# Attention output of a hybrid decoder layer: one 512-column matmul in place of two of 256 columns, and a sum of four quarters after it

## The chip, the core and the metric

The kernel is one program on one NeuronCore of a Trainium2 chip. The core has a matrix engine (PE), a vector engine (DVE), a scalar engine (ACT), a second elementwise engine (POOL) and a queue that issues most transfers (SP). Each runs its own instructions in order and they wait for each other through semaphores. The metric is the time of one execution on the device, in microseconds; lower is better. PE writes its results to PSUM, eight banks of 512 fp32 columns on 128 partitions; DVE and ACT read them from there, and POOL works on SBUF alone in this kernel.

## What is computed

One decoder layer on x (1024 x 1024, fp32): a joint projection to q, k, v (8 heads of 64) and to a gated MLP over chunks, dilated causal attention, an output projection with a layer norm, a feed-forward part with a depthwise convolution, and a gate. The part that the change touches is the attention. The reference forms three dilated windows and merges them by their denominators:

```python
scores = jnp.einsum('bnqrhd,bnkrhd->bnrhqk', qb, kb) * (1.0 / math.sqrt(dh))
scores = jnp.where(mask[None, :, None, None], scores, NEG_INF)
e = jnp.exp(scores - m)
out = jnp.einsum('bnrhqk,bnkrhd->bnqrhd', e / den, vb)
...
wts = jax.nn.softmax(jnp.stack(lses, axis=0), axis=0)
return jnp.einsum('cbsh,cbshd->bshd', wts, jnp.stack(outs, axis=0))
```

The kernel computes the same as one causal attention in which a key that lies in two or three of the windows counts two or three times (a mask that adds log 2 or log 3).

## The kernel before

To keep fp32 precision every operand is split into a high and a low part (`hi` is the value rounded by a copy, `lo` the rest), and products are summed over the parts. A linear layer takes three matmuls for this (`mm3`, L131 to L134). The program order is written out by hand: what a Python loop issues first comes first on its engine.

Attention runs over 32 units, one for each pair of a block I of 256 queries (I = 0 to 3) and a head h. A unit has I + 1 slots, so there are 80 slots. In each slot, in this order, `attention` (L743) issues: the scores of a later unit (`unit_S`, L661: two matmuls at L688 and L689 into a bank "S", of which there are two); on DVE a pass that adds the mask and finds the maximum (L698), and then whatever stands in the list `later`; the exp of a finished unit on ACT (L704) and its normalisation on POOL (L710, L712); four (in the last slot of a unit three) transposes of 128 x 128 probabilities on PE (`unit_T`, L719) into one of three banks, followed by a copy on ACT that makes the high part of the tile `pt` (L111) and, through `later`, a subtraction on DVE that makes its low part (L723); the product with V (`unit_PV`, L545) of the slot three slots back; and some matmuls of another stage (L132 to L134), with DVE work of their own (L637 splits the mixed heads, L650 adds to the residual, L579 and L583 are layer norm statistics).

`unit_PV` takes two key blocks a slot. The weights are V of one head: 64 columns of the high part and 64 of the low part, so partitions 0 to 63 of the output bank "O" hold probabilities times V high, and partitions 64 to 127 probabilities times V low. The moving operand is 256 columns of `pt` (128 for the last key block of a unit, which lies on the diagonal), once for the high and once for the low part, both summed into the same 256 columns of the bank. There are two "O" banks, and a unit holds one from its first slot to the end of its output.

After a unit's last slot `unit_out` (L560) copies one half of the partitions to SBUF with ACT (tile `ot`, L569 by way of L111) and puts a DVE addition of the other half into `later` (L570); it writes into `mixf`. It runs in the next slot, behind that slot's passes at L698 and the subtraction at L723 that were listed before it. `ot` is a tile of its own with one buffer. Most other tiles of the stage (`pt`, `sp`, `qe`, `x`) are pages of 4 KiB a partition out of one pool of 24 (`page`, L67); when no page is free, the first instruction that writes a new one waits for the last reader of the one that comes free next. After the last unit, `wo_up(3)` needs its `mixf` first (L111 and L637, then the matmul at L134), and the feed-forward stage follows.

Of the kernel before, what the change touches and what calls it, by code (L numbers as in the profile page):

```python
# [21 lines left out]
F32 = mybir.dt.float32  # L22
# [3 lines left out]
OP = mybir.AluOpType  # L26
# [25 lines left out]
def hybrid_layer(ctx, tc, x, xT, pT, pos, w_in, ln_z_g, ln_z_b, w_sT, b_sT, w_o,  # L52
# [3 lines left out]
    PE, ACT, DVE, POOL, SP = nc.tensor, nc.scalar, nc.vector, nc.gpsimd, nc.sync  # L56
# [4 lines left out]
    small = ctx.enter_context(tc.tile_pool(name="small", bufs=2))  # L61
# [5 lines left out]
    def page(shape, dt, name):  # L67
        return pool.tile(shape, dt, name=name, tag="pg", bufs=24)

    def wpage(shape, dt, name):  # L70
        return pool.tile(shape, dt, name=name, tag="w", bufs=12)
# [17 lines left out]
    def ps1(tag):  # L89
        if tag == "T":  # L90
            tag = ("D1", "B", "B")[n_t[0] % 3]
            n_t[0] += 1
        if tag == "P":
            return psL[0].tile([128, 512], F32, name=tag, tag=tag, bufs=4)
        if tag in ("S", "O"):
            return psL[0].tile([128, 512], F32, name=tag, tag=tag, bufs=2)
        return psR.tile([128, 512], F32, name=tag, tag=tag, bufs=2 if tag == "B" else 1)
# [11 lines left out]
    def copy(eng, dst, src):  # L109
        if eng is ACT:  # L110
            ACT.activation(dst, src, AF.Copy)  # L111
        else:
            eng.tensor_copy(dst, src)
# [288 lines left out]
    def vs(kb):  # L402
        if kb < 4:
            return VL[:, kb]
        if kb not in VP:
            VP[kb] = page([128, H, 128], F32R, "VP")
        return VP[kb]
# [3 lines left out]
    for j in range(4):  # L411
# [6 lines left out]
        for t in range(2):  # L418
            v = vs(2 * j + t)
# [125 lines left out]
    def unit_PV(I, h, m, pt):  # L545
        st = unit_state[I, h]
        if m == 0:
            st["o"] = ps1("O")
        o = st["o"]
        for kb in (2 * m, 2 * m + 1):  # L550
            full = kb <= 2 * I
            src = (kb - 2 * m) * 256
            osl = o[:, 0:256] if full else o[:, 128:256]
            wd = 256 if full else 128
            v = vs(kb)[:, h, :]
            for hl in range(2):
                PE.matmul(osl, v, pt[:, hl, src:src + wd], start=kb == 0 and hl == 0,
                          stop=kb == 2 * I + 1 and hl == 1)

    def unit_out(I, h):  # L560
        st = unit_state.pop((I, h))
        o = st["o"]
        p, odd = divmod(h, 2)
        if h == 0:
            mixes[I] = wpage([128, 4, 256], F32, "mixf")
        r, r2 = (slice(64, 128), slice(0, 64)) if odd else (slice(0, 64), slice(64, 128))
        ot = small.tile([128, 256], F32, name="ot", bufs=1)
        copy(ACT, ot[r], o[r2, 0:256])
        mix = mixes[I][r, p, :]  # L569
        later.append(lambda: DVE.tensor_tensor(mix, o[r, 0:256], ot[r], OP.add))  # L570

    x1 = {}
    lnp = []
# [156 lines left out]
    later = []  # L730
# [12 lines left out]
    def attention(plan):  # L743
# [5 lines left out]
        def flush(keep):  # L749
            while len(pending) > keep:  # L750
                a = pending.pop(0)
                unit_PV(*a)
                if a[2] == a[0]:
                    outs.append(a[:2])

        for n in range(-3, len(units)):
# [8 lines left out]
            for m in range(banks):  # L765
                take = -(-len(news) // (banks - m))
                ttrs = [unit_S(*units[v], ch) for v, ch in news[:take]]
                for f in ttrs + later:
                    f()
                later.clear()  # L770
                for d in [d for d in due if d[0] <= slot]:
                    due.remove(d)
                    d[2]()
                for v, ch in news[:take]:
                    if ch[3]:
                        due.append((slot + 1, "e", lambda v=v, p=ch[0]: unit_exp(*units[v], p)))
                        if ch[0] == 1:
                            due.append((slot + 2, "n", lambda v=v: unit_norm(*units[v])))
                news = news[take:]
                if n >= 0:  # L780
                    I, h = units[n]
                    pt = unit_T(I, h, m)
                    pending.append((I, h, m, pt))
                    flush(3)
                if posts and slot >= posts[0][0] and posts[0][1] in q_toks:
                    later.append(q_post(*posts.pop(0)[1:]))
                pump(rate[0])
                for o in outs:
                    unit_out(*o)
                outs.clear()  # L790
                advance()
                slot += 1
# [4 lines left out]
        for o in outs:  # L797
            unit_out(*o)
# [621 lines left out]
```

## Time and profile before

| | |
|---|---|
| median of three runs | 1275.75 us |
| the three runs | 1273.85, 1275.75, 1277.27 us |
| span of the profiled execution | 1273.2 us |
| attention in it | from about 266 to 466 us |
| busy share of the span: PE, PE weight load | 97%, 79% |
| busy share: DVE, ACT, POOL | 69%, 40%, 53% |
| DMA | 103 GB/s over the span |

The span runs from the first to the last instruction of the profiled execution; what lies around it is not in the trace. That execution lies at the fast end of the three timed runs. Matmuls are pipelined, and the duration shown for one reaches beyond the start of the next, so the cost of a matmul in a row of them is read from start to start. The number behind "x" on a row counts instructions that were merged into it; the bracket names the engine's idle time before the row and what ended it.

### The profile page before, as it was taken

What the parts mean: (1) busy time and instruction counts of PE and PEld (TensorE: products, weight loads), DVE (VectorE), ACT (ScalarE), POOL (GpSimd) and SP (SyncE); (2) the same over time, 40 slices, a digit from 0 to 9 for tenths busy, and PEclk for the clock granted to TensorE, in tenths of its full rate; (3) what the DMA queues carried; (4) which work ended last, traced back from release to release, by engine and by line L of the source; (5) the groups of instructions that cost most, each with busy time, mean ns of one, the idle gap of its engine ahead of it and who ended that gap; (6) DMA issues with size and microseconds to landing.
All of it is one profiled execution on the core that took longest, in us unless ns stands there. A gap on an engine that the chain in (4) does not pass through costs nothing. (4 is left out here: it accounts for less than half of the span.)

```text
span 1273.2 us, 15840 instructions
## 1 busy us (share of the span) xinstructions
PE 1236.7 (97%) x5804; PEld 1003.4 (79%) x5804; DVE 883.4 (69%) x1227; ACT 504.4 (40%) x855; POOL 672.9 (53%) x550
## 2 busy tenths in 40 slices
PE   9999999999999997999999999999999899989997
PEld 6888888877777777888888888888877688868886
DVE  4544422356887788777777777877779977797766
ACT  5322122366866563433333333333343344531221
POOL 2500001254737679467666767666664565783444
PEclk9999999999999998999999999999999999999998
DMA  7115511000201031033212333213688344530001
GB/s 268 67 50 181 182 53 46 34 17 1 84 34 67 34 132 67 34 124 124 93 55 101 124 125 124 100 53 129 206 279 296 104 124 156 191 124 34 34 34 50
DMA packets 61007, 131.71 MB, mean 103 GB/s; under 512 B 5377, under 2 KB 23169, under 8 KB 60929
## 3 DMA queue, kind: packets, MB, share of 16 engines
q1 hardware_dynamic: 58480, 122.17, 28.1%
q10 hardware_dynamic: 2448, 8.52, 2.1%
q8 instruction: 46, 0.75, 0.2%
q14 instruction: 33, 0.26, 0.1%
HBM read 97.90 MB, written 32.77 MB: 103 GB/s over the span
## 5 line engine op out<-in xcount | busy, mean ns | idle before, releaser
L117 POOL TENSOR_TENSOR aop<-raw,aop 128x512 fp32r<-128x512 f32 x77 | 117.6, 1537 | 81.3 <-ACT aop L111 81.2
L132 PE MATMUL P<-xop,wop 128*128 128x512 f32 (+1 forms) x360 | 138.8, 386 | 0.0
L134 PE MATMUL P<-xop,wop 128*128 128x512 f32 (+1 forms) x360 | 138.4, 384 | 0.0
L133 PE MATMUL P<-xop,wop 128*128 128x512 f32 (+1 forms) x360 | 138.4, 384 | 0.0
L117 POOL TENSOR_TENSOR wop<-s,wop 128x512 fp32r<-128x512 f32 x44 | 64.0, 1464 | 96.3 <-ACT wop L111 96.3
L117 DVE TENSOR_TENSOR bop<-wd,bop 128x512 fp32r<-128x512 f32 x66 | 85.2, 1302 | 25.8 <-ACT bop L111 25.7
L117 POOL TENSOR_TENSOR wop<-raw,wop 128x512 fp32r<-128x512 f32 x64 | 82.8, 1300 | 30.9 <-ACT wop L111 30.7
L429 POOL TENSOR_TENSOR rt<-tok,cos_t 128x128 f32<-128x128 f32 x8 | 4.7, 585 | 176.4 <-ACT tok L488 165.2
L133 PE MATMUL P<-bop,aop 128*128 128x512 f32 x176 | 71.3, 405 | 11.7 <-DVE bop L117 11.6
L111 ACT ACTIVATE wop<-s 128x512 fp32r<-128x512 f32 x44 | 26.8, 630 | 138.5 <-DVE s L936 72.3
L132 PEld LDWEIGHTS P<-xop,wop 128*128 128x128 f32 x360 | 67.7, 188 | 13.4
L134 PEld LDWEIGHTS P<-xop,wop 128*128 128x128 f32 x360 | 67.6, 188 | 13.4
L133 PEld LDWEIGHTS P<-xop,wop 128*128 128x128 f32 x360 | 67.7, 188 | 13.3
L111 ACT ACTIVATE aop<-raw 128x512 fp32r<-128x512 f32 x77 | 48.1, 625 | 74.9 <-DMA raw<-hid_d 41.9
L117 POOL TENSOR_TENSOR wop<-wraw,wop 128x512 fp32r<-128x512 f32 x44 | 73.2, 1690 | 6.4 <-ACT wop L111 4.0
L134 PE MATMUL P<-bop,aop 128*128 128x512 f32 x176 | 70.2, 399 | 3.0 <-POOL aop L117 3.0
L132 PE MATMUL P<-bop,aop 128*128 128x512 f32 x176 | 69.7, 396 | 0.0
L1022 POOL TENSOR_TENSOR ht<-ht,ct 128x1024 f32<-128x1024 f32 x22 | 63.1, 2866 | 3.9 <-ACT ht L1019 3.9
L132 PE MATMUL B<-xop,wop 128*128 128x512 f32 x160 | 62.2, 389 | 0.0
L133 PE MATMUL B<-xop,wop 128*128 128x512 f32 x160 | 62.2, 389 | 0.0
L134 PE MATMUL B<-xop,wop 128*128 128x512 f32 x160 | 62.2, 389 | 0.0
L698 DVE CUSTOM_DVE_ANT_0 sp<-S,mask 128x512 f32<-128x512 f32 (+2 forms) x64 | 37.0, 589 | 35.6 <-PE S L689 31.7
(322 smaller groups left out, 3625.7 us busy)
## 6 DMA issues: line engine op xcount, KB each, us to landing
raw<-hid_d SPq DMA_DIRECT2D x35, 512.0 KB, 3.9
hid_d<-ct SPq DMA_DIRECT2D x22, 512.0 KB, 5.2
wd<-in_w_down_dram SPq DMA_DIRECT2D x44, 256.0 KB, 5.1
raw<-in_w_in_dram SPq DMA_DIRECT2D x18, 512.0 KB, 3.7
hid_d<-ht SPq DMA_DIRECT2D x33, 256.0 KB, 5.0
raw<-in_w_a_dram SPq DMA_DIRECT2D x11, 512.0 KB, 3.5
raw<-in_w_b_dram SPq DMA_DIRECT2D x11, 512.0 KB, 4.3
wraw<-in_w_a_dram SPq DMA_DIRECT2D x11, 512.0 KB, 5.2
```

What stands on the lines that cost most here:

```text
L111: ACT.activation(dst, src, AF.Copy)
L117: lo_eng.tensor_tensor(lo, src, hi.bitcast(F32), OP.subtract)
L132: PE.matmul(ps, sh, mh, start=first, stop=False)
L133: PE.matmul(ps, sh, ml, start=False, stop=False)
L134: PE.matmul(ps, sl, mh, start=False, stop=last)
L429: POOL.tensor_tensor(r[:, 0], x1, cb, OP.mult)
L698: DVE.tensor_tensor_reduce(dst, o, mask[:, m0:m0 + w_], op0=OP.add, op1=OP.min, accum_out=acc, scale=-1.0, scalar=prev)
L1022: POOL.tensor_tensor(tt[g, e], tt[g, e], ctile[g, 1, e], OP.mult)
```

## The change

The product of a key block with V becomes one matmul of 2 x 256 columns (2 x 128 on the diagonal): the bank "O" is read as two halves, and the high part of the probabilities goes to columns 0 to 255 and the low part to columns 256 to 511. The two parts are no longer added in PSUM. `unit_out` then has four quarters to add: ACT copies 64 x 512 in place of 64 x 256, DVE adds the other 64 x 512 from PSUM to it in place, and a second DVE addition adds the two halves of 256 columns, both in SBUF. `ot` moves from its own buffer into the pool of pages.

```diff
-        o = st["o"]
+        o = st["o"].rearrange("p (l q) -> p l q", l=2)
         for kb in (2 * m, 2 * m + 1):
             full = kb <= 2 * I
             src = (kb - 2 * m) * 256
-            osl = o[:, 0:256] if full else o[:, 128:256]
             wd = 256 if full else 128
-            v = vs(kb)[:, h, :]
-            for hl in range(2):
-                PE.matmul(osl, v, pt[:, hl, src:src + wd], start=kb == 0 and hl == 0,
-                          stop=kb == 2 * I + 1 and hl == 1)
+            PE.matmul(o[:, :, 256 - wd:256], vs(kb)[:, h, :], pt[:, :, src:src + wd], start=kb == 0,
+                      stop=kb == 2 * I + 1)
...
-        ot = small.tile([128, 256], F32, name="ot", bufs=1)
-        copy(ACT, ot[r], o[r2, 0:256])
+        ot = page([128, 2, 256], F32, "ot").rearrange("p l q -> p (l q)")
+        copy(ACT, ot[r], o[r2])
         mix = mixes[I][r, p, :]
-        later.append(lambda: DVE.tensor_tensor(mix, o[r, 0:256], ot[r], OP.add))
+
+        def join():
+            DVE.tensor_tensor(ot[r], o[r], ot[r], OP.add)
+            DVE.tensor_tensor(mix, ot[r, 0:256], ot[r, 256:512], OP.add)
+        later.append(join)
```

## Rows read from the trace of the kernel before

**Rows 1.** The page's first part: busy time, share and instructions of each engine.

```profile
PE 1236.7 (97%) x5804; PEld 1003.4 (79%) x5804; DVE 883.4 (69%) x1227; ACT 504.4 (40%) x855; POOL 672.9 (53%) x550
```

**Rows 2.** Busy time by stretch of attention: length, PE, PEld, DVE, ACT, POOL, clock, DMA.

```profile
284.00:316.00 32.00, 31.67 (x162) 22.77 (x160) 20.58 (x50) 21.37 (x54) 16.32 (x29) 1.00 0.00 1
316.00:347.00 31.00, 30.75 (x177) 22.73 (x176) 25.69 (x72) 26.52 (x59) 22.79 (x31) 1.00 0.25 86
347.00:391.00 44.00, 44.00 (x231) 32.49 (x231) 33.48 (x79) 25.98 (x49) 18.81 (x25) 1.00 0.07 25
391.00:451.00 60.00, 60.00 (x329) 43.42 (x328) 44.93 (x103) 35.51 (x65) 41.00 (x44) 1.00 0.15 53
451.00:466.00 15.00, 13.61 (x104) 12.34 (x102) 13.85 (x26) 11.13 (x21) 11.41 (x12) 1.00 0.38 136
```

**Rows 3.** Timeline of PE, four places: start and duration in us, instruction.

```profile
359.98 0.48 PE L132 MATMUL D<-wouh,mixh 128*128 128x512 f32 x1
360.30 0.39 PE L133 MATMUL D<-woul,mixh 128*128 128x512 f32 x1
...
429.46 0.65 PE L557 MATMUL O<-pt,VP 128*128 128x256 f32 x4
...
429.95 0.45 PE L132 MATMUL D<-wouh,mixh 128*128 128x512 f32 x1
...
430.24 0.39 PE L133 MATMUL D<-woul,mixh 128*128 128x512 f32 x1
...
434.15 0.72 PE L557 MATMUL O<-pt,VL 128*128 128x256 f32 x4
...
434.71 0.39 PE L132 MATMUL D<-wouh,mixh 128*128 128x512 f32 x1
...
434.94 0.39 PE L133 MATMUL D<-woul,mixh 128*128 128x512 f32 x1
...
477.07 0.28 PE L132 MATMUL P<-xop,wop 128*128 128x256 f32 x1
...
478.38 0.28 PE L134 MATMUL P<-xop,wop 128*128 128x256 f32 x1
```

**Rows 4.** Groups by line and shape, 266 to 465 us: busy us, mean ns, idle before.

```profile
L570 DVE TENSOR_TENSOR mixf<-O,ot 64x256 f32<-64x256 f32 x32 | 13.4, 418 | 1.6 <-ACT ot L111 1.1
L111 ACT ACTIVATE ot<-O 64x256 f32<-64x256 f32 x32 | 12.1, 377 | 5.2 <-DVE mixf L570 3.4 <-PE O L557 1.2
L111 ACT ACTIVATE qo<-B 64x512 fp32r<-64x512 f32 x8 | 4.8, 594 | 0.1
L637 DVE TENSOR_TENSOR mixl<-mixf,mixh 128x512 fp32r<-128x512 f32 x6 | 4.7, 790 | 0.0
L468 DVE TENSOR_TENSOR ql<-B,qo 64x512 fp32r<-64x512 f32 x4 | 2.8, 694 | 0.1
```

**Rows 5.** Timeline of DVE near the start of the span.

```profile
5.45 0.42 DVE L117 TENSOR_TENSOR xl<-xraw,xh 128x256 fp32r<-128x256 f32 x1
```

**Rows 6.** Timeline of the engines in the first two stretches of rows 2.

```profile
285.65 0.42 DVE L570 TENSOR_TENSOR mixf<-O,ot 64x256 f32<-64x256 f32 x1
...
286.27 0.66 PE L557 MATMUL O<-pt,VL 128*128 128x256 f32 x4
...
327.90 0.19 PEld L688 LDWEIGHTS S<-KO,qo 128*128 128x128 f32 x1 [0.24 <-DVE pt L723]
```

**Rows 7.** Waits of the stage: engine, line and releaser, us in total, times, longest.

```profile
ACT pt L111 <- PE O L557: 5.7, 4, 2.1
```

**Rows 8.** Timeline of the engines where attention ends.

```profile
460.81 0.55 PE L719 MATMUL D<-ident,sp 128*128 128x128 f32 x3 [1.25 <-DVE pt L723]
...
463.86 0.43 DVE L570 TENSOR_TENSOR mixf<-O,ot 64x256 f32<-64x256 f32 x1 [1.06 <-ACT ot L111]
...
465.14 1.50 DVE L637 TENSOR_TENSOR mixl<-mixf,mixh 128x256 fp32r<-128x256 f32 x1
...
466.69 0.50 PE L134 MATMUL D<-wouh,mixl 128*128 128x512 f32 x1 [0.70 <-DVE mixl L637]
```

## Prediction, made before the changed kernel was run

> **What bounds the kernel now.** I read the busy shares first: PE works 97% of the span, DVE 69% [rows 1]. Such a mean says little, so next comes the table of stretches over attention, the one stage that the change touches [rows 2]. The reader is to see there that PE has next to no idle time up to 451 us, and that DVE's idle time differs by stretch: 11.4 us of 32 where block I = 0 is put out, 5.3 of 31 for I = 1, 10.5 of 44 and 15.1 of 60 for most of I = 2 and 3, and 1.2 of 15 in the drain at the end. The clock is full throughout. So PE sets the pace, except where DVE is nearly as full: in the second stretch PE already stands still for a DVE result, at the weight load at 327.90 [rows 6], and in the drain it loses 1.25 us at once to one [rows 8]. Then I read PE's timeline from start to start for the price of the product with V [rows 3], the groups by shape for the prices of the new sums [rows 4, 5], and last the two ends of the stage, where there is no queue of other work [rows 6, 8].
>
> **What PE gains.** From the first of four V matmuls to the matmul after the next one takes 0.79 us in a full slot (434.15 to 434.94) and 0.78 us in a slot with the diagonal (429.46 to 430.24). The same pair of following matmuls, without V matmuls ahead of it, takes 0.32 us (359.98 to 360.30) [rows 3]. So the four cost 0.47 and 0.46 us. A 512-column matmul costs 0.23 us (434.71 to 434.94), a 256-column one 0.12 us (477.07 to 478.38 are eleven starts) [rows 3]. After the change a full slot has two of 512 columns, 0.46 us, and gains about 0.01 us; a diagonal slot has one of each, 0.35 us, and gains 0.11 us: its 128-column matmuls cost more than their columns. With 48 full and 32 diagonal slots, PE gains 0.6 + 3.5 = 4.1 us. No row here shows a moving operand in two pieces that lie 512 columns apart; were its 512 columns to cost twice 0.12 us, the full slots would gain nothing and the sum would be 3.5 us, so little hangs on it. I take 4.1 us. Columns stay the same in number; half of the 320 instructions go.
>
> **What DVE pays.** The addition at L570 grows from 64 x 256 to 64 x 512. The same shape from PSUM takes 0.69 us at L468 against 0.42 us now: 0.28 us more [rows 4]. The second addition is new: 256 columns with both sources in SBUF took 0.42 us with POOL at rest [rows 5]. With POOL at work such instructions take longer: the six 128 x 512 ones at L637 average 0.79 us, 0.10 us above L468's [rows 4], and one of 128 x 256 at 465.14 took 1.50 us, 1.08 us above its price [rows 8]. POOL is busy for 110.3 of the 182 us of rows 2, which gives 0.65 us if each meeting costs the whole 1.08 us. Between 0.10 and 0.65 us I take 0.20, near the row with six samples. An output thus costs DVE 0.9 us more (0.8 to 1.35), 29 us for 32 outputs, beside 44 us of idle time in all of rows 2. Whether that idle time can take it has to be asked stretch by stretch.
>
> The Trainium skill speaks against this part of the change: its page "SBUF — State Buffer", section "Who interferes with whom", says that a DVE instruction with two SBUF inputs contends with a GpSimd instruction that reads SBUF, and that one with at most one SBUF input does not. By that, the change adds 32 instructions that contend, where L570 is none. The trace agrees so far (the 1.50 us above, while POOL was at work); taken at its fullest it is the third rival below.
>
> **Where it comes due.** The additions stand in DVE's queue ahead of the next slot's work: the statistics, the residual additions, then the next mask passes (which free the banks "S") and the subtractions at L723 (which free the transposes' banks, and which the next V matmuls wait for). So DVE falls 0.9 us further behind PE with each output, makes good whatever idle time it has, and PE waits once the lag is more than the margin it had.
> First stretch: eight outputs cost 7.2 us, idle time is 11.4, but at 286.27 the V matmul begins 0.20 us after the addition that frees its bank ends (285.65 + 0.42) [rows 6]. So 0.7 us come through there, and at one more place like it: 1.4 us (0 to 2).
> Second stretch: eight outputs cost 7.2 us against 5.3 us of idle time, part of it gaps between passes too short for use, and PE has no margin in its middle. Were all idle time used, 1.9 us come through; were none, 7.2. What PE gains here, 1 us, only brings it sooner to the same wait. I take 3.7 us.
> Third and fourth: twelve outputs, 10.8 us, in 25.6 us of idle time; 0.4 us for the first of them, which follows the full stretch (0 to 1).
> Drain: three outputs ahead of the last, with 1.2 us idle and PE waiting for L723: 2.7 us (1.2 to 3.6).
> Last output: its addition waits for ACT's copy, and PE's matmul at 466.69 for the split behind it [rows 8], so everything shows: 0.22 us of ACT (0.594 less 0.377 [rows 4]) and 0.9 us of DVE, 1.1 us (0.9 to 2).
> Together 9.3 us.
>
> ACT's 32 copies cost it 0.22 us each, 7 us in all beside 61 idle us in rows 2; behind a copy on ACT stand the next exps and copies to `pt`, which PE needs only three slots on, and I put nothing for them. The 3.4 us for which a copy to the single `ot` waits for the addition before it [rows 4] vanish, out of idle time, and gain nothing. The page for `ot` costs something where all 24 pages are in use. That happens now: four times a copy to `pt` waits for the V matmul that frees its page, 5.7 us in all [rows 7]. Counting first and last uses in the program's order, some five of the new copies find no free page, one at the start and four in block I = 3, and wait for a page of the next slot, at most a slot of 2.35 us each (429.46 to 434.15 are two [rows 3]). In the fourth stretch ACT is idle for 24.5 of 60 us, so I put nothing; it is the fourth rival.
>
> **The sum.** 9.3 us lost less 4.1 gained is 5.2 us more. The profiled execution would go from 1273.2 to 1278.4 us. That span lies 2.5 us under the median of the three runs, 1275.75, which I take as the base: 1281.0 us. What follows attention begins with the outputs of that last matmul and is bound by PE, so nothing takes the delay back.
>
> **The rivals.** First, the idle time covers it (not slower): if DVE can use its idle time up to 451 us in full, only drain and last output remain, 3.8 us against 4.1 gained: 1275.5 us. The point that decides is 5.3 / 8 = 0.66 us for an output in the second stretch; my 0.9 is above it, but the margins ahead of that stretch may stretch it. For it speaks that PE waits little for DVE now; against it that it waits at all where both are full. Second, the drain hides its outputs too, because the wider matmuls let PE arrive later and wait less: then 0.3 us remain of the losses and the time is 1272.0. Against it stands the wait at 460.81. Third, POOL makes each second addition wait: at 1.35 us for an output the stretches give about 2.3, 8, 1, 4 and 2 us, less 4.1: 1289 us. For it speaks the 1.50 us row; against it the mean of 0.79 us. Fourth, the copies that wait for pages hold ACT so long that `pt` comes late: about half of five slots, 6 us on top, 1287 us; the idle time of ACT and the three slots speak against it.
>
> **How the numbers follow.** The forecast has a chance of 0.50, with its own range from 1277 to 1285 us. The first rival has 0.28, the second 0.06, the third 0.11, the fourth 0.05. A measurement can tell 0.3%, 3.8 us: faster is below 1271.9, slower above 1279.6. Faster is the second rival, 0.06. Within 0.3% are the first and about a quarter of the forecast, 0.40. Slower is the rest, 0.54. The range from 1274.0 to 1287.0 takes in the forecast, most of the first rival, the fourth, and about half of the third; outside are the second and what is left, some 0.16.
>
> **What would show it.** In the changed kernel's trace L557 has 160 matmuls, and from their start to the matmul after the next takes 0.78 us in a full slot and 0.67 in a diagonal one. The two additions take 0.69 and 0.42 to 0.8 us; a mean near 1 us for the second speaks for the third rival. In 316 to 347 us, DVE is full and PE has idle time "<- DVE" of some 3 us; if it has none, the first rival holds. The matmul that waits for L637 waits about a microsecond more. If PE's waits for DVE up to 451 us stay as they are, or if the next matmul after a diagonal slot comes no sooner, the prediction's steps are wrong.

## The result, and the profile of the changed kernel

The changed kernel takes 1291.43 us (median of four runs, 1290.09 to 1293.88) against 1276.26 us for the kernel before in the same comparison: a ratio of 1.0124, interval 1.0109 to 1.0139. The forecast was 1281.0 us with a range up to 1287.0. It is slower, as forecast, but by 15.2 us in place of 5.2. The profiled execution has a span of 1288.4 us, 15.2 us above that of before, so the two traces hold the whole difference.

The page's first part, to be set beside [rows 1]: PE has 160 matmuls fewer, DVE 32 instructions and 26 us more.

```profile
PE 1241.1 (96%) x5644; PEld 995.4 (77%) x5644; DVE 909.3 (71%) x1259; ACT 511.5 (40%) x855; POOL 673.4 (52%) x550
```

The same stretches as in [rows 2], of the changed kernel, with the same columns (length, PE, PEld, DVE, ACT, POOL, clock, DMA):

```profile
284.00:316.00 32.00, 31.26 (x144) 21.68 (x143) 26.35 (x58) 23.82 (x56) 16.22 (x29) 1.00 0.00 1
316.00:347.00 31.00, 29.67 (x115) 19.78 (x114) 25.17 (x61) 22.17 (x46) 20.54 (x26) 0.78 0.16 47
347.00:391.00 44.00, 42.60 (x201) 29.64 (x199) 39.69 (x92) 29.07 (x56) 16.82 (x24) 1.00 0.15 52
391.00:451.00 60.00, 59.53 (x276) 40.34 (x276) 50.51 (x111) 36.76 (x63) 41.97 (x45) 1.00 0.15 53
451.00:466.00 15.00, 14.21 (x86) 10.79 (x84) 12.61 (x26) 10.86 (x19) 10.79 (x13) 1.00 0.00 0
```

The reader is to look at the column ahead of the DMA share: in 316 to 347 us the granted clock is 0.78, where it was 1.00 before. PE is busy for 29.67 of 31 us and yet gets through 115 matmuls where it got through 177; about 30 of the difference are the change's own, four V matmuls of a slot having become two, and the rest is speed. Busy time alone would have hidden this.

Where the 15.2 us arise is read by setting the start of the same PE instruction (all but those of the product with V) in one trace against the other. In the third column stands the forecast, its losses less the part of PE's 4.1 us that falls in that stretch (0.11 for a diagonal slot, 0.01 for a full one).

| stretch (times of before) | delay added, measured | forecast |
|---|---|---|
| up to 284 us | +0.3 | 0 |
| first, 284 to 316 | -0.2 | +0.5 |
| second, 316 to 347 | +6.7 | +2.7 |
| third and fourth, 347 to 451 | +0.4 | -1.2 |
| drain and last output, 451 to 470 | +7.8 | +3.2 |
| all that follows | +0.1 | 0 |

So two places make the loss, by 4.0 and 4.6 us more than forecast. The first is read in one timeline, of POOL, DVE and PE together (start, duration, instruction; the bracket is idle time and what ended it):

```profile
323.96 1.28 POOL L537 TENSOR_TENSOR woul<-raw,wouh 128x512 fp32r<-128x512 f32 x1 [0.29 <-ACT wouh L111]
...
324.24 1.28 DVE L570 TENSOR_TENSOR mixf<-ot 64x256 f32<-64x256 f32 x1
...
325.45 0.67 DVE L699 CUSTOM_DVE_ANT_0 sp<-S,mask 128x512 f32<-128x512 f32 x1
...
326.19 0.50 PE L689 MATMUL S<-KE,qe 128*128 128x512 f32 x1 [1.33 <-DVE nmx L699]
```

The second addition meets a POOL instruction and takes 1.28 us, ending 0.3 us after that one. The mask pass behind it on DVE is late, the bank "S" comes free late, and PE stands still for 1.33 us. The stretches before and after that moment show what follows:

```profile
316.00:326.60 10.60, 9.27 (x45) 6.03 (x43) 9.97 (x24) 8.78 (x19) 8.39 (x14) 1.00 0.00 0
326.60:340.20 13.60, 13.60 (x39) 9.37 (x39) 9.09 (x25) 8.15 (x17) 7.88 (x10) 0.50 0.11 40
```

For 13.6 us after the wait PE runs at half its clock, 1.2 GHz of 2.4; then the clock is full again. The delay grows from -0.1 us at 323.3 us to +1.4 at 325 (the wait) and to +7.1 at 333. The second place is the drain, here as PE's waits of the stretch 444 to 486 us (in total, times, longest), the last four outputs:

```profile
PE D L134 <- DVE mixl L638: 1.9, 1, 1.9
PE D L132 <- ACT mixh L111: 1.3, 1, 1.3
PE B L720 <- DVE pt L724: 1.1, 1, 1.1
PE D L720 <- DVE pt L724: 1.1, 1, 1.1
PE S L861 <- DVE xop L869: 0.8, 1, 0.8
PE O L554 <- DVE pt L724: 0.3, 1, 0.3
```

That is 6.5 us, where [rows 8] has 1.25 and 0.70. The remainder, some 3 us, is clock again:

```profile
470.00:473.40 3.40, 3.15 (x9) 2.04 (x8) 3.12 (x5) 1.65 (x4) 3.25 (x3) 0.50 1.00 340
473.40:480.20 6.80, 3.51 (x14) 2.29 (x14) 5.35 (x6) 1.53 (x3) 6.64 (x6) 1.00 0.64 260
480.20:483.60 3.40, 3.40 (x8) 2.69 (x9) 2.84 (x3) 0.00 (x0) 1.01 (x1) 0.50 0.48 158
```

The prices themselves came out as forecast. The two sums, grouped by shape over 266 to 490 us, answer to [rows 4] and [rows 5]:

```profile
L569 DVE TENSOR_TENSOR ot<-O,ot 64x512 f32<-64x512 f32 x32 | 21.9, 685 | 2.0 <-ACT ot L111 1.4
L570 DVE TENSOR_TENSOR mixf<-ot 64x256 f32<-64x256 f32 x32 | 18.5, 577 | 1.1
```

An output costs DVE 685 + 577 - 418 = 844 ns more (forecast 0.9 us). PE's timeline answers to [rows 3], a diagonal slot and a full one:

```profile
427.92 0.59 PE L554 MATMUL O<-pt,VP 128*128 128x512 f32 x2
428.35 0.40 PE L132 MATMUL D<-wouh,mixh 128*128 128x512 f32 x1
428.58 0.39 PE L133 MATMUL D<-woul,mixh 128*128 128x512 f32 x1
...
434.76 0.71 PE L554 MATMUL O<-pt,VP 128*128 128x512 f32 x2
435.30 0.39 PE L132 MATMUL D<-wouh,mixh 128*128 128x512 f32 x1
435.53 0.40 PE L133 MATMUL D<-woul,mixh 128*128 128x512 f32 x1
```

From the V matmul to the matmul after the next it is 0.66 us with the diagonal (0.78 before, 0.67 forecast) and 0.77 us in a full slot (0.79 before, 0.78 forecast).

### The profile page after: what moved, and what is told of

The parts are those of the page before. It is cut to its first block, busy times and chain, and to the rows that moved or that the text cites. A ratio compares the mean times of both kernels' runs of the same rounds, so it can differ in the third digit from the quotient of the medians.

```text
span 1288.4 us, 15557 instructions
## 1 busy us (share of the span) xinstructions
PE 1241.1 (96%) x5644; PEld 995.4 (77%) x5644; DVE 909.3 (71%) x1259; ACT 511.5 (40%) x855; POOL 673.4 (52%) x550
## 5 line engine op out<-in xcount | busy, mean ns | idle before, releaser
L111 ACT ACTIVATE wop<-raw 128x512 fp32r<-128x512 f32 x66 | 41.1, 627 | 42.1 <-PE B L134 25.5
```

## Experiments

Two theories stood against each other at first. The clock theory: the added sums make DVE late at a few places, PE stands still there, and the larger loss is the half clock after it. The queue theory: the work in DVE's queue sets the loss by itself, output by output, and the clock is a bystander. Beside them the forecast's page rival (ACT held up by the new pages for `ot`). Line numbers in the rows are those of each kernel and shift by one or two, or by some twelve, with its edit.

**The two halves of the change, each alone.** The wide matmul with the single sum of before (the product with the low part of the probabilities is not added):

```diff
-        ot = page([128, 2, 256], F32, "ot").rearrange("p l q -> p (l q)")
-        copy(ACT, ot[r], o[r2])
+        ot = small.tile([128, 256], F32, name="ot", bufs=1)
+        copy(ACT, ot[r], o[r2, 0:256])
...
-            DVE.tensor_tensor(ot[r], o[r], ot[r], OP.add)
-            DVE.tensor_tensor(mix, ot[r, 0:256], ot[r, 256:512], OP.add)
...
+        later.append(lambda: DVE.tensor_tensor(mix, o[r, 0:256], ot[r], OP.add))
```

> The wide matmuls of the change with the copy, the single addition and the ot of before; the sum leaves out the product with the low part of the probabilities. It measures PE's gain alone: 4.1 us by the starts of matmuls, so 1272 us in every theory; 1276 us or more if the wide matmuls themselves upset something, 1268 us or less if the gain is larger than the starts show.

Measured: 1271.25 us against 1275.53, ratio 0.9968 (0.9956 to 0.9979): 4.3 us less. Its profiled execution, the slowest of the seven, has 3.4 us at half clock in attention too (335.2 to 338.6 us), behind a PE wait of 0.52 us at 334.25. And the four-quarter sums with the narrow matmuls of before, high and low part side by side in the bank:

```diff
-            PE.matmul(o[:, :, 256 - wd:256], vs(kb)[:, h, :], pt[:, :, src:src + wd], start=kb == 0,
-                      stop=kb == 2 * I + 1)
+            for hl in range(2):
+                PE.matmul(o[:, hl, 256 - wd:256], vs(kb)[:, h, :], pt[:, hl, src:src + wd],
+                          start=kb == 0 and hl == 0, stop=kb == 2 * I + 1 and hl == 1)
```

> The narrow matmuls of before, 256 and 128 columns, but into two halves of the bank, with the copy and both additions of the change. It measures the price of the sums alone. Theory of the queue: DVE has the same work and PE 4 us more, 1291 to 1295 us. Theory of the clock: PE has more to do ahead of each wait, so DVE is less behind it: the wait at block I = 1 is shorter than 1.3 us and the clock may hold; then 1282 to 1287 us, otherwise 1291 to 1295 us. Theory of the pages: 1293 to 1295 us.

Measured: 1295.85 us, ratio 1.0156 (1.0125 to 1.0188): 20.3 us more, 0.85 us above the top of all three theories, so it doesn't tell them apart. The halves add up within the spread of its four runs (1290.8 to 1299.31): 20.3 - 4.3 = 16.0 for the 15.2 of the whole. The gain of PE was sized right, the cost of the sums was put at 9.3 us and is 20.3. In this kernel's trace the meeting with POOL is another, a little later, with the same sequel: a second addition of 1.25 us beside POOL's 1.29 and, some microseconds on, the weight load that waits for DVE, at the end of which the clock falls to 0.50, for 20.5 us. A PE wait of 1.12 us before it, at 327.42, is followed by full clock.

```profile
335.51 1.29 POOL L537 TENSOR_TENSOR woul<-raw,wouh 128x512 fp32r<-128x512 f32 x1 [0.70 <-ACT wouh L111]
335.83 1.25 DVE L571 TENSOR_TENSOR mixf<-ot 64x256 f32<-64x256 f32 x1
...
340.48 0.29 PEld L690 LDWEIGHTS S<-KE,qe 128*128 128x128 f32 x1 [1.88 <-DVE nmx L700]
```

The stretch after it, with the columns of [rows 2]:

```profile
340.20:360.70 20.50, 20.22 (x66) 15.06 (x67) 13.91 (x35) 10.12 (x21) 6.62 (x8) 0.50 0.32 103
```

**The second addition elsewhere.** First with one source in PSUM, so that it does not meet POOL (one quarter is left out, another taken twice):

```diff
-            DVE.tensor_tensor(mix, ot[r, 0:256], ot[r, 256:512], OP.add)
+            DVE.tensor_tensor(mix, o[r, 256:512], ot[r, 0:256], OP.add)
```

> The changed kernel, but the second addition reads the bank's columns 256 to 511 in place of the second half of ot, so it has one source in PSUM; the sum leaves out one of the four quarters and takes one twice. DVE's number and size of instructions are the same. Theory of the clock (one second addition that waits for POOL, 1.28 us at 324 us, lets PE stand still for 1.33 us, and the granted clock falls to half for 13.65 us there): the second addition takes 0.42 us everywhere, no half-clock stretch between 316 and 347 us, 1279 to 1283 us. Theory of the queue (DVE's extra work alone does it, meetings with POOL matter little): 22 of the 27 us of extra DVE work remain, 1287 to 1291 us, with the half-clock stretch. Theory of the pages (the copies to ot that wait for a page): unchanged, 1291 us.

Measured: 1284.02 us, ratio 1.0064 (1.0046 to 1.0082), nearer to the clock theory, though 1 us above its bound. All 32 additions take 422 ns now, DVE's queue is 0.16 us an output shorter, 5 us in all, and the loss against before falls from 15.2 to 8.5 us. No half clock is left in 316 to 347 us; one of 3.4 us in the drain is.

Then on POOL, away from DVE:

```diff
-            DVE.tensor_tensor(mix, ot[r, 0:256], ot[r, 256:512], OP.add)
+            POOL.tensor_tensor(mix, ot[r, 0:256], ot[r, 256:512], OP.add)
```

> The changed kernel with the second addition on POOL: DVE pays 0.27 us more for an output in place of 0.84 us. Clock and queue theories: PE's waits for DVE in block I = 1 fall to those of the kernel before, no half-clock stretch there, and PE's gain of 4 us shows in part: 1273 to 1279 us, with up to 1.5 us lost behind the last output, where POOL is busy. Theory of the pages: 1289 us or more.

Measured: 1298.04 us, ratio 1.0176 (1.0161 to 1.0191). The clock and queue theories missed this, because neither had looked at what is queued behind the addition on its new engine. The page theory's "1289 us or more" holds by the number, but not for its reason, as the waits show. The waits of POOL and PE over 266 to 480 us:

```profile
POOL mixf L570 <- DVE ot L569: 44.3, 14, 8.8
...
PE D L720 <- POOL sp L713: 5.4, 6, 2.4
```

POOL stands still for DVE's first addition, up to 8.8 us, with the normalisation of the next probabilities (L713) behind it, and PE's transposes wait for that. Five stretches at half clock, 24 us in all, lie between 289 and 485 us in this kernel.

**One late place in the kernel before.** This takes the change away and keeps one suspected cause. The addition of one output of block I = 1 is issued seven times (same values):

```diff
-        later.append(lambda: DVE.tensor_tensor(mix, o[r, 0:256], ot[r], OP.add))
+        for _ in range(7 if (I, h) == (1, 2) else 1):
+            later.append(lambda: DVE.tensor_tensor(mix, o[r, 0:256], ot[r], OP.add))
```

> The kernel before, with one change: at one output of block I = 1, head 2 (the addition L570 at about 323 us) the addition is issued seven times in a row instead of once, writing the same values; everything else is as before. That is 6 x 0.42 = 2.5 us of DVE work more, at one place. Clock theory (PE that stands still for DVE for more than about a microsecond is given half its clock for some time after, and that costs several times the stall): PE loses 1.3 to 2 us at its next mask pass and then some 4 us in a stretch at granted clock 0.5, so 5 to 8 us more than before, 1281 to 1284 us, with a half-clock stretch that begins between 324 and 330 us. Queue theory (only the work in DVE's queue counts; the clock falls for reasons of its own): at most the 2.5 us less DVE's idle time nearby, 1 to 2 us more, 1277 to 1278 us, no half clock there.

Measured: 1284.12 us against 1276.21, ratio 1.0067 (1.0051 to 1.0083): 2.5 us of DVE work cost 7.9 us. DVE and PE around the place:

```profile
323.94 3.11 DVE L571 TENSOR_TENSOR mixf<-O,ot 64x256 f32<-64x256 f32 x7
...
327.70 0.49 PE L689 MATMUL S<-KE,qe 128*128 128x512 f32 x1 [1.91 <-DVE nmx L699]
```

The stretch after it:

```profile
328.10:341.70 13.60, 13.60 (x47) 10.26 (x47) 7.60 (x23) 7.58 (x18) 6.93 (x8) 0.50 0.13 39
```

Against the trace of before the delay is +0.8 us from 200 to 323 us, +2.9 at 325, +8.7 at 333, and then +8.3 without a change up to 497 us. So the stall cost 2.1 us and the half clock after it 5.4 us, at one place. The four runs, 1281.59 to 1284.88 us, all lie above the highest of before (1277.88). This is the clearest run of the study. The same with four issues in place of seven:

```diff
-        for _ in range(7 if (I, h) == (1, 2) else 1):
+        for _ in range(4 if (I, h) == (1, 2) else 1):
```

> As e5_one_late_place, but with the addition issued four times in place of seven: 3 x 0.42 = 1.26 us of DVE work more at the same output. There PE had a margin of 0.6 us (in the kernel before the bank of the scores at 324.87 us is free at 324.25). Clock theory with an onset (a stall of 1.9 us is followed by half clock, one of 0.6 us is not): PE waits 0.6 us and that is all, 1276 to 1277.5 us. Rival: every stall of PE there, however short, is followed by a stretch at half clock: 1279 to 1283 us.

Measured: 1278.14 us against 1275.89, ratio 1.0021 (1.0008 to 1.0033), 0.6 us above the upper bound of the clock theory and below the rival's. The trace has the short stall (first fence, PE) and the full clock behind it (second, a stretch); the delay grows by 0.8 us there and by nothing up to 490 us. One of the ten executions was not like this: 1284.87 us at a mean granted clock of 0.986, where the other nine have 0.990 to 0.994 and the kernel with seven issues 0.987. It has no trace, so where its clock fell is not known.

```profile
326.71 0.50 PE L689 MATMUL S<-KE,qe 128*128 128x512 f32 x1 [0.56 <-DVE nmx L699]
```

```profile
326.00:340.00 14.00, 13.19 (x75) 9.52 (x74) 11.75 (x35) 12.52 (x27) 12.17 (x14) 1.00 0.37 130
```

Half of the extra work cost about a quarter by the medians (2.2 of 7.9 us) and a tenth by the traces (0.8 of 7.5): at this place the price is no straight line in DVE's work. The seven issues once more, at an output of block I = 2, where DVE has idle time:

```diff
-        for _ in range(7 if (I, h) == (1, 2) else 1):
+        for _ in range(7 if (I, h) == (2, 4) else 1):
```

> As e5_one_late_place with the same seven additions, but at an output of block I = 2 (head 4, between 375 and 392 us), where DVE has idle time before its next pass. If idle time ahead of the next pass and the free bank take most of the 2.5 us: PE waits 0 to 1 us, no half clock, 1276 to 1277.5 us. If a late DVE costs as much there as in block I = 1: 1283 to 1285 us.

Measured: 1276.87 us, ratio 1.0009 (1.0000 to 1.0019). PE waits 0.75 us once, the clock stays full in 347 to 391 us, and the delay grows by 1.0 us. There the forecast's reasoning by idle time holds.

```profile
382.26 3.10 DVE L571 TENSOR_TENSOR mixf<-O,ot 64x256 f32<-64x256 f32 x7
...
386.01 0.50 PE L132 MATMUL D<-wouh,mixh 128*128 128x512 f32 x1 [0.75 <-DVE x L651]
```

**Can the second stretch be mended in the changed kernel?** First by the one addition that met POOL at 324 us:

```diff
-            DVE.tensor_tensor(mix, ot[r, 0:256], ot[r, 256:512], OP.add)
+            a, b = (ot, o) if (I, h) == (1, 2) else (ot, ot)
+            DVE.tensor_tensor(mix, a[r, 0:256], b[r, 256:512], OP.add)
```

> The changed kernel, with only the second addition of block I = 1, head 2 (the one at 324.24 us that took 1.28 us beside a POOL instruction) reading one source from PSUM in place of SBUF; that one output leaves out one of its four quarters and takes another twice. Clock theory: the addition takes 0.42 us, PE's wait at 326.2 us falls from 1.33 to some 0.4 us, and the half-clock stretch at 326.6 us goes: 5 to 7 us less than the changed kernel, 1284 to 1286 us, though one instruction of 15557 was changed. If the next long meeting with POOL in block I = 1 brings the same stretch a little later, 1290 to 1292 us with a half-clock stretch at another place. Queue theory: 0.9 us less at most, 1290.5 us.

Measured: 1296.8 us, ratio 1.0162 (1.0137 to 1.0187). All numbers missed. The trace shows the expected sequel at the place, and the same trouble 14 us later:

```profile
323.63 1.28 POOL L537 TENSOR_TENSOR woul<-raw,wouh 128x512 fp32r<-128x512 f32 x1 [0.30 <-ACT wouh L111]
...
323.89 0.41 DVE L571 TENSOR_TENSOR mixf<-ot,O 64x256 f32<-64x256 f32 x1
...
338.13 0.50 PE L690 MATMUL S<-KE,qe 128*128 128x512 f32 x1 [1.79 <-DVE nmx L700]
```

And the stretch after the last of these rows:

```profile
340.10:357.10 17.00, 17.00 (x49) 11.68 (x48) 11.97 (x28) 8.79 (x18) 4.75 (x6) 0.50 0.30 97
```

Beside the very same POOL instruction the addition takes 0.41 us in place of 1.28; at 333 us the delay against before is +0.8 us where the changed kernel has +7.1. But five more outputs of that block follow, two of them meet POOL again (second additions of 1.26 us at 333.48 and 0.79 at 336.56), and the next stall was longer and the half clock after it too. Taking one place away helps only if no other is waiting. Second, by keeping PE occupied:

```diff
+                pre = None
+                if n >= 0 and units[n][0] == 1:
+                    pre = ps1("T")
+                    PE.matmul(pre, vs(0)[:, 0, :], KE[:, 0, 0:512], start=True, stop=True)
...
-                    pt = unit_T(I, h, m)
+                    pt = unit_T(I, h, m, pre)
```

> The changed kernel with PE work that nobody needs added in block I = 1: ahead of each slot's scores, one more matmul of 128 x 512 into the bank that the slot's transposes then overwrite, 16 of them, 0.23 us each, 3.7 us of PE in all. DVE's work is unchanged. Clock theory: PE arrives later, waits less for DVE, and no half clock follows in 316 to 351 us, so the kernel loses 3.7 us and gets back the 1.4 us wait and some 5.5 us of half clock: 1286 to 1290 us, faster than the changed kernel's 1291.4 though it does more. Queue theory: DVE's lag is what sets the second stretch, so PE's extra work hides in the waits in part and the time is 1291 to 1295 us.

Measured: 1293.44 us, ratio 1.0154 (1.0112 to 1.0195), by the number the queue theory's case. By the trace it is mixed: the 3.7 us of added work do hide for the most part (0.6 to 1.0 us behind the changed kernel from 350 to 484 us, of which 1.0 was there before the added work began), the stall at 326 us is gone, and a new one stands 14 us later, followed by 3.4 us of half clock in place of 13.6. From 484 to 521 us it falls back by another 2.4 us, with longer stretches at half clock. Its four executions differ with the clock: 1289.49 us at a mean granted clock of 0.994, 1293.24 and 1293.64 at 0.988, 1302.56 at 0.977; the first lies in the clock theory's range. The median does not tell the theories apart.

```profile
341.94 0.50 PE L689 MATMUL S<-KE,qe 128*128 128x512 f32 x1 [1.61 <-DVE nmx L699]
```

**The pages.** The kernel before with `ot` as a page of the pool:

```diff
-        ot = small.tile([128, 256], F32, name="ot", bufs=1)
+        ot = page([128, 256], F32, "ot")
```

> The kernel before with one change: the tile ot (128 x 256) is a page of the pool of 24 in place of a buffer of its own. Page theory (the fourth rival: copies that wait for pages hold ACT and make the probabilities late): 3 to 6 us more than before, 1279 to 1282 us. Clock and queue theory: ACT waits more for pages (about twice the 5.7 us of before), PE does not notice: within 1 us of before, 1275 to 1277 us.

Measured: 1276.52 us against 1276.21, ratio 1.0008 (0.9998 to 1.0019). ACT waits more for pages than in [rows 7], and PE hardly waits for ACT (0.2 us, as before). In the changed kernel the same wait of ACT's comes to 10.0 us between 266 and 490 us, and the only long wait of PE's for ACT is the 1.3 us behind the last output, where ACT itself waits for DVE. The fourth rival falls. The wait, over 266 to 500 us:

```profile
ACT pt L111 <- PE O L557: 7.9, 6, 2.1
```

**The old code at the tight places.** The changed kernel with the narrow matmuls and the single sum for the last four outputs alone, and then (with `I != 1 and` in the first line of `wide`) for block I = 1 as well:

```diff
+    def wide(I, h):
+        return (I, h) < (3, 4)
...
+            if wide(I, h):
...
+            else:
+                for hl in range(2):
+                    PE.matmul(o[:, 0, 256 - wd:256], vs(kb)[:, h, :], pt[:, hl, src:src + wd],
+                              start=kb == 0 and hl == 0, stop=kb == 2 * I + 1 and hl == 1)
...
+            if w == 256:
+                DVE.tensor_tensor(mix, o[r, 0:256], ot[r, 0:256], OP.add)
+                return
```

> The changed kernel, in which only the last four outputs keep the matmuls and the single sum of the kernel before. Clock theory with the loss placed by the two traces (6.9 us in the second stretch, 7.8 in drain and last output): 1291.4 - 7.8 = 1283.6 us, with the half clock near 326 us still there; 1281 to 1286. If the drain's loss is a consequence of the delay in the second stretch and not of its own sums: 1289 to 1292 us.

Measured: 1282.3 us, ratio 1.0060 (1.0040 to 1.0081), 9.1 us less than the changed kernel. The drain's waits are those of [rows 8] again, and the delay stays at +6.1 us from 451 to 470 us. The two half-clock stretches of the drain are gone as well. So the drain's loss is made by its own four sums and does not follow from the delay before it.

```profile
466.87 0.55 PE L732 MATMUL D<-ident,sp 128*128 128x128 f32 x3 [1.21 <-DVE pt L736]
472.80 0.50 PE L134 MATMUL D<-wouh,mixl 128*128 128x512 f32 x1 [0.64 <-DVE mixl L650]
```

> The changed kernel, in which the outputs of block I = 1 and the last four outputs of block I = 3 (12 of 32) keep the matmuls and the single sum of the kernel before; the other 20 have the wide matmul and the sums of four quarters. Clock theory (the loss arises at the two places where DVE has no idle time, there by waits and the half clock that follows them): both losses vanish and the remainder stands where the traces put it, +0.1 in the first stretch and +0.4 in the third and fourth: 1276 to 1277.5 us, no half clock between 316 and 460 us. Queue theory with lag carried along: the twenty outputs that still cost DVE 0.84 us more bring a third of the loss, 1279 to 1282 us. Were the PE gain of 0.11 us for each of 20 diagonal slots to come through whole, 1274 us.

Measured: 1277.27 us against 1275.89, ratio 1.0009 (1.0000 to 1.0018). The loss is gone but for 1.4 us, and attention runs at full clock throughout:

```profile
316.00:347.00 31.00, 30.76 (x167) 22.18 (x166) 25.73 (x71) 27.08 (x60) 22.53 (x30) 1.00 0.26 86
347.00:391.00 44.00, 43.08 (x199) 29.83 (x199) 37.88 (x83) 26.15 (x49) 17.85 (x25) 1.00 0.07 25
```

Twenty outputs with the change give PE some 2.5 us by the forecast's prices, and none of it arrives: in 347 to 380 us alone the delay grows by 1.0 us, with 0.9 us of idle PE in 347 to 391. Even where DVE has idle time, the sums cost what the matmul gains. A version of the change that beats the kernel before was not found.

## Why the prediction was right or wrong

**PE's gain, 4.1 us: right.** Alone it is 4.3 us, and both slot prices agree. The operand in two pieces costs no more than one of 512 columns.

**DVE's price, 0.9 us an output: right,** 0.844 measured; the meetings with POOL add 577 - 420 = 0.16 us in the mean, put at 0.20.

**"The clock is full throughout": the step that failed.** It was read off the kernel before, for which it is true up to 466 us, and carried over into a sum in which PE was made to stand still. Every term of "where it comes due" counted a microsecond of PE's waiting as a microsecond. In the second stretch the forecast's loss, 3.7 us (1.9 to 7.2), became 7.7 (the 6.7 of the table and PE's 1.0): about 1.4 us of wait at one place and the rest after it, at half clock. The forecast's own sign was a full DVE and some 3 us of PE's waits in 316 to 347 us; there PE waits 1.33 us and DVE is busy for 25.17 of 31. That a late DVE result at that place brings the half clock is shown by the seven issues in the kernel before, where nothing else was changed; that the second stretch would otherwise cost little is shown by the kernel with the narrow code there. An estimate from these traces: the changed kernel spends 20.5 us at half clock between 316 and 484 us; at the 0.4 us for each microsecond that the seven issues show, that is some 8 of the 10 us by which the forecast fell short. The trace of before had a warning, which was not read because it lies behind attention: after 3.1 us in which PE is idle, out of 8.3, comes a stretch at half clock.

```profile
483.00:491.30 8.30, 5.20 (x44) 4.99 (x43) 7.43 (x5) 2.24 (x4) 8.06 (x8) 1.00 0.16 63
491.30:498.10 6.80, 5.57 (x26) 5.57 (x27) 6.80 (x7) 2.61 (x6) 6.80 (x6) 0.50 0.00 0
```

**Drain 2.7 and last output 1.1: mis-sized, 8.4 in all** (7.8 and PE's 0.6). The upper bounds were 3.6 and 2. Some 4.5 us are waits beyond those of before, some 3 us the half clock in two pieces; the rest has no row of its own. The third rival is a part of it, which the sum had priced at the mean: three of the four second additions of the drain take 1.00, 0.95 and 1.44 us, not 0.62, beside a busy POOL (6.64 of 6.80 us in the second row of the table of the drain). It is the smaller part: with one source in PSUM, where each takes 0.42 us, drain and last output still add 5.6 us. Behind the last output, the split that PE waits for stands in DVE's queue after a subtraction with two SBUF sources, which takes 1.66 us (first row, the changed kernel) where it took 0.90 (second, before); the forecast had no term for it.

```profile
477.01 1.66 DVE L839 TENSOR_TENSOR tc<-x 128x512 f32<-128x512 f32 x1
...
464.32 0.90 DVE L838 TENSOR_TENSOR tc<-x 128x512 f32<-128x512 f32 x1
```

**First stretch, 1.4 us gross:** 0.7 measured (-0.2 and PE's 0.9). The forecast set the whole 0.9 us against 0.20 us of margin at the bank "O". But only the first addition reads the bank, so it is free 0.27 us later than before and not 0.9. At the place that the forecast named no wait of PE's shows: the addition ends at 286.79 us and the V matmul starts at 286.83. The one wait stands at another output, 0.72 us at 306.88 (first row, one of PE's waits in 284 to 400 us), where the kernel before waits 0.33 (second row). The loss was smaller than forecast, and came by another way.

```profile
PE O L554 <- DVE ot L569: 0.7, 1, 0.7
...
306.64 0.71 PE L557 MATMUL O<-pt,VL 128*128 128x256 f32 x4 [0.33 <-DVE mixf L570]
```

**Third and fourth stretch, 0.4 us gross:** about 2.0 (0.4 and PE's 1.6). Idle time takes a single late addition of 2.5 us with 1 us lost, but twelve longer outputs cost more than one.

**The rivals.** The first (idle time covers it) falls: the second stretch lost. The point at which it was to decide, 0.66 us an output, is nearly that of the run with one source in PSUM, 0.69 us, and there the stretch from 316 to 347 us added 1.7 us without a half clock, 2.7 with PE's 1.0, where idle time used in full would have let 0.2 through. So the idle time covers less than its sum. The second falls with the drain. The third had the right mechanism and the wrong form: not each addition was slow, the mean is 0.58 us, but a few were, and one of 1.28 us began the costly chain. The Trainium skill's rule on its page "SBUF — State Buffer", section "Who interferes with whom", that was set beside it agrees with the runs: beside the same POOL instruction the addition took 1.28 us with two SBUF sources and 0.41 with one. The fourth falls.

**What stays open.** When a wait is followed by the half clock, and for how long. Its length alone does not decide. One instruction waits 0.74 us in the changed kernel (first row) and keeps the full clock; in the kernel with one output from PSUM it waits 0.74 us (second row) and 3.4 us at half clock follow from 391.3 us.

```profile
387.49 0.44 PE L689 MATMUL S<-KE,qe 128*128 128x384 f32 x1 [0.74 <-DVE nmx L699]
...
390.09 0.44 PE L690 MATMUL S<-KE,qe 128*128 128x384 f32 x1 [0.74 <-DVE nmx L700]
```

The wait of 1.33 us at 326 us is followed by 13.6 us at half clock in the changed kernel and by 10.2 us in the one with the old code in the drain. Another instruction of the second stretch waits 1.73 us (the sums alone), 1.79 (one output from PSUM), 1.61 (PE kept busy) and 0.52 us (the wide matmul alone), and 20.5, 17.0, 3.4 and 3.4 us at half clock go with it. Waits of 1.25 us in the kernel before [rows 8] and of 1.12 us with the sums alone are followed by full clock. So the mark of about a microsecond in the clock theory is not what the runs show. The traces do not settle what else decides, and so the two runs that tried to mend the second stretch could not be forecast to a few microseconds.

## What to carry to other kernels

Where PE is the bound, a microsecond that it waits in the middle of dense work can cost several: look for the places at which one late result stops it at once, and price them with the clock after the stall as a range, from nothing to several times the stall, since equal stalls had different sequels here. An addition that is moved between engines or lengthened is sized by the longest of its kind beside a busy POOL, at the tight places, and by the mean only where there is slack. And a move to another engine is a move into another queue: what stands behind the instruction there waits with it.

## What the runs showed of the hardware

- In the block of the second stretch the granted clock fell to 0.50 at PE stalls of 0.5 to 1.9 us, for 3.4 to 20.5 us in different kernels; after others of 0.56, 1.12 and 1.25 us in attention it stayed full. At one clean place a stall of 1.91 us was followed by 13.6 us at half clock, which cost 5.4 us: 0.4 us for each microsecond of it, less than the half that a clock halved would suggest.
- A DVE addition with two SBUF sources that starts beside a running POOL instruction that reads SBUF ends some 0.3 us after it (1.28, 1.25 and 1.00 us in place of 0.42); with one source in PSUM it does not (0.41 us).
- A moving operand of two pieces of 256 columns that lie apart costs what 512 in a row cost (two such and the next two matmuls take 0.77 us; forecast from 512 in a row, 0.78).
